# A hybrid decoder layer: the compression's position blocks become the stationary operand in fp32r halves, and the first norm sums by transposes

## The chip, the cores and the metric

The kernel runs on one core of one Trainium2 chip. The metric is the device time of one execution in microseconds (us); three runs of the kernel before gave 677.79, 677.90 and 678.41 us, so the median is 677.9. Engines are named as in the profile: PE (TensorE matmuls), PEld (TensorE weight loads), DVE (VectorE), ACT (ScalarE), POOL (GpSimd) and SP (SyncE, which only issues transfers here).

## What is computed

One decoder layer on a residual stream of 512 tokens and 1024 features in fp32. The first RMS norm feeds one large projection; its parts go to a pooling mixer, to a sparse attention with three key/value branches (compressed, selected, window) and to two merge gates; then come the output projection, a second norm and a gated MLP with a three-tap convolution. The change touches two places of it.

The norm:

```python
y = xf * lax.rsqrt(jnp.mean(xf * xf, axis=-1, keepdims=True) + RMS_EPS)
```

The compression, once for the keys and once for the values. A block is 32 consecutive tokens, a new block starts every 16, so there are 31 blocks of each of 2 groups:

```python
blk = kv[:, idx] + pe[None, None, :, None, :]
hid = jax.nn.silu(jnp.einsum('bnlgd,ldh->bngh', blk, w1))
return jnp.einsum('bngh,hd->bngd', hid, w2)
```

The sum over 32 positions of 64 features is a contraction over 2048 numbers; the kernel stores two positions on top of each other in the 128 partitions, which leaves 16 steps of 128 (position pairs). `w1` has 128 columns per step.

## The kernel before

**Precision.** Nearly all matmuls run on fp32r operands. A tensor is split by `split` into a rounded high half (an ACT copy to fp32r) and the rest (a DVE subtraction), and a product is three matmuls: high by high, high by low, low by high. A few small products stay plain fp32; the profile shows each of them as two MATMUL rows. Every MATMUL has a weight load (PEld) of its own.

**Stages.** The program begins with eight steps of the query/key projection (`round_a`), with the first norm's column sums made in between (`norm_rstd`, called at step 6 of 8). Then follow two streams that share all engines. The main stream "m" transposes queries and keys, computes the two compressions, the compressed attention and eight heads of attention. The filler stream "f" computes 22 feature tiles (`feature`: eight steps of three matmuls with 512 columns, "mm<-xh,whi", "mm<-xl,whi" and "mm<-xh,wlo" in the rows): two of them (`kv_in`) are the inputs of the compressions, the others feed the pooling mixer and the gates. After both streams come the output products and the MLP.

**Order.** All calls are recorded by `Plan` first. Each instruction gets a price (`Plan.price`, for a matmul its moving columns over 2250, at least 0.109 us), and a list scheduler searches for an order of the five engines in which PE, which takes its two streams each in their program order, has little to wait for. The order that it found is then emitted, and each engine runs it as it stands. A changed call can therefore move instructions that have nothing to do with it. Every instruction has line 434 in the profile (the line that emits), so the rows are told apart by tile names.

**First norm.** `square_x` adds the squares of the eight feature tiles into `acc` (128 features by 512 tokens). `norm_rstd` multiplies each 128-token slice of `acc` (stationary) by one column of ones, four plain fp32 matmuls with one moving column, and DVE turns the sums into `rstd` in 12 tiny steps.

**Compression.** `kv_in(i)` multiplies the feature tile by the broadcast norm into `kc` and adds the position table `pe` twice, once for the first half of a block's positions and once for the second: two tiles `kcb`, whose last axis is the position pair. Then, for 16 position pairs, a 128x128 piece of `w1` is stationary and the 62 block columns move, all plain fp32, into 62 columns of one bank. Tanh on ACT and one DVE step make `hid`, and a small matmul by `w2` follows (`compress_out`, "tr<-pr,hid").

## Time and profile before

| | |
|---|---|
| median of the three runs | 677.9 us |
| profiled execution | 678.3 us, of which its span 676.5 us |
| granted TensorE clock | 0.999 |
| PE / PEld busy in the span | 670.7 us / 610.1 us |
| DVE / ACT / POOL busy | 559.5 us / 467.3 us / 111.9 us |
| MATMUL rows | 4366 |

The span is cut by the profiler from the first to the last instruction. The rows of PE overlap, because a matmul's end is modelled: a row of 0.39 us may stand only 0.23 us after the one before. What a matmul costs PE is read from the distance of starts, or from a count of rows in a stretch in which PE never pauses. The two compressions lie at 71.8 to 75.4 us and 78.2 to 82.0 us, the first norm's sums at 30.7 to 31.5 us, and the two streams run until about 272 us.

### The profile page before, as it was taken

What the parts mean: (1) busy time and instruction counts of PE and PEld (TensorE: products, weight loads), DVE (VectorE), ACT (ScalarE), POOL (GpSimd) and SP (SyncE); (2) the same over time, 40 slices, a digit from 0 to 9 for tenths busy, and PEclk for the clock granted to TensorE, in tenths of its full rate; (3) what the DMA queues carried; (4) which work ended last, traced back from release to release, by engine and by line L of the source; (5) the groups of instructions that cost most, each with busy time, mean ns of one, the idle gap of its engine ahead of it and who ended that gap; (6) DMA issues with size and microseconds to landing.
All of it is one profiled execution on the core that took longest, in us unless ns stands there. A gap on an engine that the chain in (4) does not pass through costs nothing.

```text
span 676.5 us, 12188 instructions
## 1 busy us (share of the span) xinstructions
PE 670.7 (99%) x4366; PEld 610.1 (90%) x4366; DVE 559.5 (83%) x1246; ACT 467.3 (69%) x877; POOL 111.9 (17%) x138
## 2 busy tenths in 40 slices
PE   9999999999999999999999999999999999999998
PEld 8898888888888888988899999999999999999997
DVE  6869778788878867788888898888888989989883
ACT  7576577777677765447787867667766877776651
POOL 0010111010110110001322312222222322321121
PEclk9999999999999999999999999999999999999999
DMA  8468646454565555847878859777877888785574
GB/s 307 146 156 265 172 109 187 96 140 117 139 165 125 143 153 174 303 148 214 235 150 180 194 130 231 176 179 165 200 168 167 173 217 183 165 181 158 145 183 110
DMA packets 51180, 117.47 MB, mean 174 GB/s; under 512 B 5808, under 2 KB 9264, under 8 KB 51120
## 3 DMA queue, kind: packets, MB, share of 16 engines
q1 hardware_dynamic: 32112, 76.44, 35.5%
q0 software_dynamic: 18864, 40.12, 32.8%
q8 instruction: 34, 0.56, 0.3%
q14 instruction: 26, 0.21, 0.1%
q10 hardware_dynamic: 144, 0.14, 0.1%
HBM read 70.28 MB, written 6.29 MB: 113 GB/s over the span
## 4 chain that ended last, share of the span: by engine, by line
PE 93%; DMA 4%; issue 2%; DVE 0%; POOL 0%; ACT 0%; POOLq 0%
PE mm L434 39%; PE tr L434 33%; PE sc L434 11%; PE av L434 11%; DMA sl<-r 2%; DMA r<-wup 1%; DMA sl<-wraw 1%; DVE ft L434 0%; POOL sl L434 0%; ACT whi L434 0%; DVE wraw L434 0%; DVE s L434 0%; DVE o L434 0%; POOLq L434 0%; POOL ones L434 0%
## 5 line engine op out<-in xcount | busy, mean ns | idle before, releaser
L434 ACT ACTIVATE whi<-wraw 128x1024 fp32r<-128x1024 f32 (+4 forms) x99 | 91.7, 929 | 35.8 <-PE sc L434 14.2
L434 DVE TENSOR_TENSOR wlo<-wraw,whi 128x1024 fp32r<-128x1024 f32 (+3 forms) x73 | 73.9, 1016 | 4.4 <-ACT whi L434 3.7
L434 PE MATMUL tr<-tl,sh 128*128 128x256 f32 x261 | 73.2, 280 | 0.0
L434 PE MATMUL tr<-th,sl 128*128 128x256 f32 x250 | 70.5, 282 | 1.2 <-DMA sl<-r 1.2
L434 PE MATMUL mm<-xh,whi 128*128 128x512 f32 x176 | 70.8, 402 | 0.0
L434 PE MATMUL tr<-th,sh 128*128 128x256 f32 x250 | 70.5, 282 | 0.0
L434 PE MATMUL mm<-xh,wlo 128*128 128x512 f32 x176 | 68.8, 391 | 0.0
L434 PE MATMUL mm<-xl,whi 128*128 128x512 f32 x176 | 68.6, 390 | 0.0
L434 POOL DMA_DIRECT2D sl<-r x46 | 39.7, 863 | 143.9 <-ACT sl L434 109.6
L434 POOL DMA_DIRECT2D wlo<-wraw x26 | 22.3, 859 | 230.7 <-ACT wlo L434 178.6
L434 PEld LDWEIGHTS tr<-tl,sh 128*128 128x128 f32 x261 | 49.2, 189 | 0.2
L434 PEld LDWEIGHTS tr<-th,sl 128*128 128x128 f32 x250 | 47.0, 188 | 1.4 <-DMA sl<-r 1.4
L434 PEld LDWEIGHTS tr<-th,sh 128*128 128x128 f32 x250 | 47.0, 188 | 0.7 <-ACT tr L434 0.2
L434 ACT ACTIVATE wlo<-wraw 128x1024 fp32r<-128x1024 f32 x26 | 27.6, 1060 | 21.2 <-PE mm L434 19.7
L434 POOL DMA_DIRECT2D sl<-wraw x30 | 25.9, 864 | 87.3 <-ACT sl L434 64.7
L434 PEld LDWEIGHTS mm<-xh,wlo 128*128 128x128 f32 x176 | 33.0, 188 | 7.3
L434 PEld LDWEIGHTS mm<-xl,whi 128*128 128x128 f32 x176 | 33.1, 188 | 6.1
L434 PEld LDWEIGHTS mm<-xh,whi 128*128 128x128 f32 x176 | 33.1, 188 | 6.0
L434 ACT ACTIVATE sh<-wraw 128x512 fp32r<-128x512 f32 x56 | 34.8, 621 | 4.3 <-DVE wraw L434 4.0
L434 ACT ACTIVATE pp<-pp,asm 128x256 f32<-128x256 f32 (+3 forms) x64 | 35.4, 557 | 3.0 <-DVE asm L434 2.7
L434 DVE SCALAR_TENSOR_TENSOR ft<-fg,pr,ft 128x511 f32<-128x511 f32 (+1 forms) x44 | 32.9, 747 | 3.1 <-ACT ft L434 2.7
L434 ACT ACTIVATE sl<-r 128x512 fp32r<-128x512 f32 x46 | 28.6, 622 | 5.1 <-DMA r<-wdz 2.6
(451 smaller groups left out, 2179.8 us busy)
## 6 DMA issues: line engine op xcount, KB each, us to landing
wlo<-wraw POOLq DMA_DIRECT2D x26, 512.0 KB, 4.6
wraw<-wup SPq DMA_DIRECT2D x23, 512.0 KB, 4.2
sl<-r POOLq DMA_DIRECT2D x46, 256.0 KB, 5.3
wraw<-wf SPq DMA_DIRECT2D x22, 512.0 KB, 3.6
r<-wup SPq DMA_DIRECT2D x42, 256.0 KB, 5.3
sl<-wraw POOLq DMA_DIRECT2D x30, 256.0 KB, 4.6
wraw<-wdn SPq DMA_DIRECT2D x16, 320.0 KB, 3.9
sl<-s POOLq DMA_DIRECT2D x17, 256.0 KB, 5.4
```

The source lines that it names most:

```text
L434: getattr(self.real[o.eng], method)(*a, **kw)
```

## The change

In the first norm each of the four slices of `acc` is transposed by the identity instead (128 columns), and DVE sums the four groups of 128 columns and then goes on as before. The second norm keeps the matmuls by ones.

In the compression the operands change places. `kc` plus the first half of the position table is laid out with the position pair first and the 64 (group, 16-token half block) columns last, and split into fp32r halves that stand side by side: a stationary of 64 high and 64 low columns for each of 8 position pairs. The weights are laid out on the host so that pair l and pair l+8 stand side by side: 256 moving columns, split on the chip into high (`w1h`) and low (`w1l`). A matmul with 256 columns therefore gives four results at once: high and low halves of the blocks, each by the first-half and the second-half weights. Two matmuls (high weights, low weights) for each of 8 pairs make 16. The 128x256 result is copied out (`ab`), its two halves are transposed back, high and low parts are added, and the two half-block sums are added with a shift of one block. As only the first half of the position table was added, the difference for the second half (`dpe`) times the weights is summed on DVE (`dsum`, 8 steps of 128 columns) and reduced over the partitions by one matmul with ones. The prices of the plan are as they were.

```diff
-    def norm_rstd(acc_tile, dst, pt):
-        with pl.unit():
-            for t in range(NT):
-                PE.matmul(pt[:, t:t + 1], acc_tile[:, t * P:(t + 1) * P], ones[:, 0:1], start=True, stop=True)
+        if turn:
+            with pl.unit():
+                for t in range(NT):
+                    PE.transpose(pt[:, t * P:(t + 1) * P], acc_tile[:, t * P:(t + 1) * P], ident)
+            DVE.tensor_reduce(v[:, 1], pt.rearrange("p (t n) -> p t n", t=NT), axis=AX, op=ALU.add)
+            DVE.tensor_scalar(v[:, 0], v[:, 1], 1.0 / D, EPS, op0=ALU.mult, op1=ALU.add)
...
+            b = page("kcb", (P, 8, 64))
+            with pl.behind(flipped[1]):
+                DVE.tensor_add(b, kc.rearrange("p g (n l) -> p l (g n)", l=8),
+                               pe[:, i, 0:8][:, :, None].to_broadcast([P, 8, 64]))
             for a in range(2):
-                b = page("kcb", (P, 2, 32, 8))
-                with pl.behind(flipped[1]):
-                    DVE.tensor_add(b.rearrange("p g n l -> p (g n) l"), kc.rearrange("p g (n l) -> p (g n) l", l=8),
-                                   pe[:, i, 8 * a:8 * a + 8][:, None, :].to_broadcast([P, 64, 8]))
-                KC[i, a] = b
+                KC[i, a] = page("kcs", (P, 4, 2, 64), F32R)
+                split(KC[i, a][:, :, 0], KC[i, a][:, :, 1], b[:, 4 * a:4 * a + 4])
...
         pt = bank("tr")
+        more = page("dsum")
+        dsum, dpe = more[:, 0:P], more[:, P:P + 8]
+        DVE.tensor_sub(dpe, pe[:, i, 8:16], pe[:, i, 0:8])
         for q in range(4):
-            with pl.unit():
-                for l in range(4 * q, 4 * q + 4):
-                    PE.matmul(pt[:, 0:62], w1t[l // 4][:, (l % 4) * P:(l % 4 + 1) * P],
-                              KC[i, l // 8][:, :, l // 8:l // 8 + NB, l % 8], start=(l == 0), stop=(l == 15))
-        ph = pt[:, 0:62].rearrange("p (g n) -> p g n", g=2)
+            hi, lo = page("w1h", dt=F32R), page("w1l", dt=F32R)
+            split(hi, lo, w1t[q])
+            for l in range(2 * q, 2 * q + 2):
+                c = slice((l % 2) * 256, (l % 2 + 1) * 256)
+                x = w1t[q][:, (l % 2) * 256 + P:(l % 2 + 1) * 256]
+                if l:
+                    DVE.scalar_tensor_tensor(dsum, x, dpe[:, l:l + 1], dsum, op0=ALU.mult, op1=ALU.add)
+                else:
+                    DVE.tensor_scalar_mul(dsum, x, dpe[:, l:l + 1])
+                w = KC[i, l // 4][:, l % 4].rearrange("p s n -> p (s n)")
+                with pl.unit():
+                    for m in (hi, lo):
+                        PE.matmul(pt[:, 0:256], w, m[:, c], start=(l == 0 and m is hi), stop=(l == 7 and m is lo))
+        ab = page("ab")[:, 0:256]
+        ACT.activation(ab, pt[:, 0:256], AF.Copy)
+        pt = bank("tr")
+        with pl.unit():
+            for a in range(2):
+                PE.transpose(pt[:, a * P:(a + 1) * P], ab[:, a * P:(a + 1) * P], ident)
+            PE.matmul(pt[:, 256:257], dsum, ones[:, 0:1], start=True, stop=True)
+        low = page("ab")
+        halves = pt[:, 0:256].rearrange("p (a s n) -> p a s n", a=2, s=2)
+        lows, sums2 = (low[:, o:o + P].rearrange("p (a n) -> p a n", a=2) for o in (0, P))
+        ACT.activation(lows, halves[:, :, 1], AF.Copy)
+        ACT.activation(low[:, 320:321], pt[:, 256:257], AF.Copy)
+        DVE.tensor_add(sums2, halves[:, :, 0], lows)
...
+        DVE.scalar_tensor_tensor(ph, a4, low[:, 320:321], b4, op0=ALU.add, op1=ALU.add)
...
-                norm_rstd(acc, rstd2, bank("sc", (P, 2, T))[:, 0])
+                norm_rstd(acc, rstd2, bank("sc", (P, 2, T))[:, 0], False)
...
+    A["w1"] = A["w1"].reshape(2, P, 2, 8, P).transpose(0, 1, 3, 2, 4).reshape(2, P, 16, P)
```

The order moves with it, in three places. On PE, at the end of the sixth step of `round_a`, the four sums by ones become four transposes ("cs" holds the identity) in the same place:

```order
 L434 MATMUL sc<-wlo,xh 128x256 x4
-L434 MATMUL mm<-ones,acc 128x1 x4
+L434 MATMUL mm<-cs,acc 128x128 x4
 L434 MATMUL tr<-whi,xh 128x512 x3
 L434 MATMUL av<-whi,xh 128x512
```

Nothing else of PE moved there. In the whole first part of PE's order, up to the last key transpose before the compressions, this is the only difference.

On DVE, where the compressions begin ("kc" is the scaled feature tile, "qt" and "kt" are halves of transposed queries and keys for the main stream), before:

```order
L434 TENSOR_TENSOR qt<-tr,qt 64x512 x2
L434 TENSOR_TENSOR kc<-mm,rb 64x256 x4
L434 TENSOR_TENSOR kcb<-kc,pr 128x512 x2
L434 TENSOR_TENSOR qt<-tr,qt 64x512 x2
L434 TENSOR_TENSOR kc<-mm,rb 64x256 x4
L434 TENSOR_TENSOR kcb<-kc,pr 128x512 x2
L434 SCALAR_TENSOR_TENSOR hid<-hth,tr 128x2x31
L434 TENSOR_TENSOR kt<-tr,kt 64x512 x2
```

and now:

```order
L434 TENSOR_TENSOR kc<-mm,rb 64x256 x4
L434 TENSOR_TENSOR kcb<-kc,pr 128x512
L434 TENSOR_TENSOR qt<-tr,qt 64x512 x2
L434 TENSOR_TENSOR w1l<-w_399,w1h 128x512
L434 TENSOR_TENSOR kcs<-kcb,kcs 128x4x64
L434 TENSOR_TENSOR w1l<-w_400,w1h 128x512
L434 TENSOR_TENSOR w1l<-w_401,w1h 128x512
L434 TENSOR_TENSOR kcs<-kcb,kcs 128x4x64
L434 TENSOR_TENSOR kc<-mm,rb 64x256 x4
L434 TENSOR_TENSOR w1l<-w_402,w1h 128x512
L434 TENSOR_TENSOR kcb<-kc,pr 128x512
L434 TENSOR_SCALAR dsum<-w_399,dsum 128x128
```

The first `kc` now stands two `qt` steps earlier in DVE's order, and from it to the second `hid` there are 65 DVE instructions, where there were 27.

On PE the first compression before stands in one piece:

```order
L434 MATMUL mm<-xh,wlo 128x512
L434 MATMUL tr<-kcb,w_397 128x62 x4
L434 MATMUL tr<-kcb,w_398 128x62 x4
L434 MATMUL tr<-kcb,w_399 128x62 x4
L434 MATMUL tr<-kcb,w_400 128x62 x4
L434 MATMUL mm<-xh,whi 128x512
```

Now it begins one filler step (three matmuls) later, and pauses after its first four matmuls for four filler steps:

```order
L434 MATMUL mm<-xh,wlo 128x512
L434 MATMUL tr<-w1h,kcs 128x256
L434 MATMUL tr<-w1l,kcs 128x256
L434 MATMUL tr<-w1h,kcs 128x256
L434 MATMUL tr<-w1l,kcs 128x256
L434 MATMUL mm<-xh,whi 128x512
```

After the other twelve come eleven filler steps, the transposes and the sum of `dsum`, the second compression's sixteen matmuls in one piece, six filler steps, its transposes and the small product by the first `hid`, seven filler steps, and the product by the second `hid`. Before, four filler steps stood between the two compressions and four between the two products by `hid`. From there on the filler stream is ahead of where it was; after the last head five filler steps are left instead of twelve. From the output products on, PE's order is the same.

More of the change, by code (lines that the diff above doesn't have):

```diff
@@ L598, in hybrid_layer, with norm_rstd @@
     rb = keep("rb", (P, T))
-    def norm_rstd(acc_tile, dst, pt):
-        with pl.unit():
-            for t in range(NT):
-                PE.matmul(pt[:, t:t + 1], acc_tile[:, t * P:(t + 1) * P], ones[:, 0:1], start=True, stop=True)
+    def norm_rstd(acc_tile, dst, pt, turn):
         v = page("nrv", (P, 2, NT))
-        DVE.tensor_scalar(v[:, 0], pt[:, 0:NT], 1.0 / D, EPS, op0=ALU.mult, op1=ALU.add)
+        if turn:
[6 more added lines that the diff above has]
+            with pl.unit():
+                for t in range(NT):
+                    PE.matmul(pt[:, t:t + 1], acc_tile[:, t * P:(t + 1) * P], ones[:, 0:1], start=True, stop=True)
+            DVE.tensor_scalar(v[:, 0], pt[:, 0:NT], 1.0 / D, EPS, op0=ALU.mult, op1=ALU.add)
         rsqrt(dst, v[:, 0], v[:, 1])
@@ L629, in hybrid_layer @@
                 square_x(j)
-            norm_rstd(acc, rstd, bank("mm"))
+            norm_rstd(acc, rstd, bank("mm"), True)
             DVE.tensor_scalar_mul(rhalf, rstd, 0.5)
@@ L900, in hybrid_layer @@
         pt = bank("tr")
+        more = page("dsum")
+        dsum, dpe = more[:, 0:P], more[:, P:P + 8]
+        DVE.tensor_sub(dpe, pe[:, i, 8:16], pe[:, i, 0:8])
         for q in range(4):
-            with pl.unit():
-                for l in range(4 * q, 4 * q + 4):
-                    PE.matmul(pt[:, 0:62], w1t[l // 4][:, (l % 4) * P:(l % 4 + 1) * P],
-                              KC[i, l // 8][:, :, l // 8:l // 8 + NB, l % 8], start=(l == 0), stop=(l == 15))
-        ph = pt[:, 0:62].rearrange("p (g n) -> p g n", g=2)
+            hi, lo = page("w1h", dt=F32R), page("w1l", dt=F32R)
[5 more added lines that the diff above has]
+                    DVE.scalar_tensor_tensor(dsum, x, dpe[:, l:l + 1], dsum, op0=ALU.mult, op1=ALU.add)
+                else:
+                    DVE.tensor_scalar_mul(dsum, x, dpe[:, l:l + 1])
[6 more added lines that the diff above has]
+        pt = bank("tr")
+        with pl.unit():
+            for a in range(2):
[7 more added lines that the diff above has]
+        DVE.tensor_add(sums2, halves[:, :, 0], lows)
+        ph = low[:, 256:318].rearrange("p (g n) -> p g n", g=2)
+        a4, b4 = (sums2[:, a].rearrange("p (g n) -> p g n", g=2)[:, :, a:a + NB] for a in range(2))
+        DVE.scalar_tensor_tensor(ph, a4, low[:, 320:321], b4, op0=ALU.add, op1=ALU.add)
         hid = keep("hid", (P, 2, 32), bufs=2)
```

## The prediction

> **What bounds the kernel now.** I read the page first, then PE's waits, then the stretches around the changed places.
>
> ```profile
> PE 670.7 (99%) x4366; PEld 610.1 (90%) x4366; DVE 559.5 (83%) x1246; ACT 467.3 (69%) x877; POOL 111.9 (17%) x138
> ...
> PE 93%; DMA 4%; issue 2%; DVE 0%; POOL 0%; ACT 0%; POOLq 0%
> ...
> PE tr L434 <- DMA sl<-r: 1.2, 1, 1.2
> PE mm L434 <- POOL ones L434: 1.0, 1, 1.0
> PE sc L434 <- DMA sl<-wraw: 0.2, 1, 0.2
> ```
>
> The last three rows are all that PE waited for: 2.4 us of 676.5. PE makes 93% of the chain that ended last. So the time is the sum of what PE issues, and an edit gains what it takes from PE, as long as DVE and ACT still feed PE. They are the second thing to look at, above all where the compressions stand. The next rows are stretches of time, each with its length and then the busy time of PE, PEld, DVE, ACT and POOL:
>
> ```profile
> 66.00:96.00 30.00, 30.00 (x174) 25.62 (x173) 21.64 (x63) 20.30 (x42) 4.41 (x6) 1.00 0.51 125
> 96.00:255.00 159.00, 159.00 (x850) 134.35 (x849) 128.75 (x398) 117.16 (x254) 15.37 (x18) 1.00 0.56 143
> 544.00:561.00 17.00, 17.00 (x126) 16.14 (x125) 15.95 (x29) 13.84 (x25) 4.51 (x6) 1.00 0.86 201
> 646.00:663.00 17.00, 17.00 (x146) 17.00 (x145) 13.82 (x28) 8.62 (x16) 5.18 (x6) 1.00 0.78 173
> ```
>
> Around the compressions DVE is free for 8.4 of 30 us and ACT for 9.7; during the heads DVE is at 81%. In the third row, in the MLP, DVE is at 94% and PE still does not pause.
>
> **What PE loses and gains.** First the old pieces and the rows that price the new ones (PE in order of time: start, length, count):
>
> ```profile
> 30.69 0.95 PE L434 MATMUL mm<-ones,acc 128*128 128x1 f32 x8
> 31.50 0.94 PE L434 MATMUL tr<-whi,xh 128*128 128x512 f32 x3
> ...
> 32.98 0.86 PE L434 MATMUL tr<-whi,xl 128*128 128x512 f32 x3
> ...
> 40.46 0.29 PE L434 MATMUL mm<-bh,xh 128*128 128x280 f32 x1
> ...
> 41.48 0.29 PE L434 MATMUL mm<-bh,xl 128*128 128x280 f32 x1
> ...
> 59.09 0.60 PE L434 MATMUL tr<-cs,kp 128*128 128x128 f32 x4
> 59.53 0.60 PE L434 MATMUL tr<-cs,qp 128*128 128x128 f32 x4
> 59.88 0.48 PE L434 MATMUL mm<-xh,whi 128*128 128x512 f32 x1
> 60.20 0.39 PE L434 MATMUL mm<-xl,whi 128*128 128x512 f32 x1
> 60.43 0.39 PE L434 MATMUL mm<-xh,wlo 128*128 128x512 f32 x1
> ...
> 71.82 3.81 PE L434 MATMUL tr<-kcb,w 128*128 128x62 f32 x32
> 75.39 0.48 PE L434 MATMUL mm<-xh,whi 128*128 128x512 f32 x1
> 75.71 0.39 PE L434 MATMUL mm<-xl,whi 128*128 128x512 f32 x1
> ...
> 85.17 0.33 PE L434 MATMUL tr<-pr,hid 128*64 128x64 f32 x2
> ```
>
> A normal 512-column matmul takes 0.23 us from start to start (60.20 to 60.43). The eight rows of the norm's sums take 31.50 - 30.69 = 0.81 us, plus 0.08 that the group behind them is longer (0.94 against 0.86): 0.89 us, 0.11 each. Eight transposes take 60.20 - 59.09 - 0.23 = 0.88 us, again 0.11 each. Four transposes for eight such rows save 4 x 0.11 = **0.45 us**.
>
> One compression takes 75.39 - 71.82 = 3.57 us and makes the matmul behind it 0.09 longer (0.32 to the next start instead of 0.23): 3.66 us for 32 rows, 0.11 each, though only 62 columns move. So one, 62 and 128 moving columns cost the same here. For 256 columns the row of 646 to 663 us gives 17.00 / 146 = 0.116 us; that stretch holds the last output products, nothing but 256-column matmuls. The new compression is 16 x 0.116 = 1.86 us, two transposes and the two rows of one plain fp32 matmul with one column, 4 x 0.11 = 0.44, and 0.09 behind them: 2.39 us. Two compressions save 2 x (3.66 - 2.39) = **2.54 us**. Together PE issues 28 matmul rows and 3.0 us less. The price of the 16 is bounded by 0.11 from below and, if the doubled stationary or the changing bank cost something, by 0.13 from above (the 280-column products: eight starts from 40.46 to 41.48): 3.1 to 2.5 us.
>
> [...]
>
> **What DVE and ACT gain, and whether it is covered.** Prices, in groups by tile (busy time, mean ns of one, idle time before):
>
> ```profile
> L434 DVE TENSOR_TENSOR qt<-tr,qt 64x512 fp32r<-64x512 f32 x8 | 5.5, 689 | 0.4 <-ACT qt L434 0.2
> L434 DVE TENSOR_TENSOR kc<-mm,rb 64x256 f32<-64x256 f32 x8 | 3.4, 422 | 0.1
> L434 DVE TENSOR_TENSOR kcb<-kc,pr 128x512 f32<-128x512 f32 x4 | 2.6, 687 | 0.1
> L434 DVE TENSOR_TENSOR kp<-kp,gkv 128x256 f32<-128x256 f32 x4 | 1.5, 420 | 0.0
> 34.65 1.14 DVE L434 SCALAR_TENSOR_TENSOR diag<-cs,rstd,diag 128x128 fp32r<-128x128 f32 x4
> 39.74 1.28 DVE L434 TENSOR_REDUCE small<-qp 128x8 f32<-128x512 f32 x2 [2.70 <-ACT qp L434]
> 68.29 1.73 DVE L434 TENSOR_TENSOR kc<-mm,rb 64x256 f32<-64x256 f32 x4
> 82.33 0.22 DVE L434 TENSOR_SCALAR kcx<-tr 64x64 f32<-64x64 f32 x1 [4.25 <-PE tr L434]
> 59.29 1.06 ACT L434 ACTIVATE wlo<-wraw 128x1024 fp32r<-128x1024 f32 x1 [3.40 <-PE mm L434]
> 64.07 1.20 ACT L434 ACTIVATE qt<-tr 64x512 fp32r<-64x512 f32 x2
> L434 ACT ACTIVATE pwh<-pw 128x512 fp32r<-128x512 f32 x1 | 0.6, 624 | 0.0
> L434 ACT ACTIVATE hth<-tr 128x62 f32<-128x62 f32 x2 | 0.4, 223 | 4.7 <-PE tr L434 4.7
> ```
>
> In the norm DVE gets a reduction of 128x512 (0.64 by the row of two) ahead of its small steps, and 16-column work of 0.4 us. The row at 39.74 shows what covers them: DVE sits idle for 2.70 us before that point, where it waits for the projection's end. Cost nothing; without that cover 1.0 us.
>
> Per compression DVE loses one `kcb` (0.69) and gets two `kcs` (0.42 each), four `w1l` (0.69), eight `dsum` (1.14 / 4 = 0.285), one 128-column sum and one 62-column step (0.29 and 0.21): +5.7 us. ACT gets four `w1h` (0.62), two `kcs` and one `ab` (0.42 each, between the 62- and the 512-wide row) and two small copies (0.3 and 0.2): +4.3 us. Two compressions bring 11.4 us to DVE and 8.5 us to ACT, against 8.4 and 9.7 us that are free between 66 and 96. It does not fit there, and the new order answers by putting filler steps of 0.68 us in front of the late work. Whether the places suffice follows from the order and these durations, place by place:
>
> *First matmuls.* DVE's first `kc` stood at 68.29; two `qt` less before it (1.38) and the norm (0.45) put it at 66.5. Then 1.73 (`kc`), 0.69 (`kcb`), 1.38 (two `qt`), 0.69 and 0.42 make 71.4. PE comes there at 71.82 + 0.68 - 0.45 = 72.05: 0.6 us to spare. On ACT the first `w1h` falls into the 3.40 us of idle time before 59.29, so it stands at its two `qt` at 63.6 instead of 64.07; these (1.2), three 1024-wide steps (1.06), three `w1h` and a `kcs` follow, and its part is there at 70.3.
>
> *Fourth group.* PE is there 0.47 + 2.73 (four filler steps) + 0.93 later, at 76.2; DVE has two `w1l`, a `kcs`, the second `kc` and the last `w1l` to do, 4.2 us, and is done at 75.6.
>
> *Sum of `dsum`, second matmuls.* Its last matmuls, eleven filler steps (7.5 us) and the two transposes bring PE to 84.4. DVE has eight `dsum`, seven 512-wide steps and a `kcs` to do, 7.5 us, and is there at 83.1; the second compression's last weights follow 1.8 us later, at 84.9, and PE wants them at 86.2.
>
> *Second `hid`.* Six filler steps, the transposes and seven more bring PE to 96.2. DVE has 5 us to do until the first `hid` (90, wanted at 91.3) and 4.3 us from there to the second: 94.3. Before, PE was at that product at 85.2: the main stream starts its heads 11 us later.
>
> So everything is in time, by 0.6 to 1.9 us, with DVE hardly pausing for 25 us and ACT little more. The chain for the second `hid` has its seven filler steps (4.8 us) for three ACT and three DVE steps of 0.2 to 0.3 us each. Behind each late instruction on PE stands the filler stream as well as the main one, since PE takes its order as it stands, so a late DVE step costs its full lateness once. The spare times come from sums of means; I take **0.5 us** as lost here, with 0 and 2.5 us as ends (2.5: each of the five products late by 0.5 us).
>
> One price has no row: the new `kcb` reads `kc` with a step of eight elements in its innermost axis. `kc` itself reads with a step of two elements at the full rate (422 ns for 256 against 420 of `kp`). I bound it by nothing and by a doubling, +0.69 us per compression, and take nothing, the nearest row; the upper end makes the first place late by 0.1 us and eats the same from the two that follow.
>
> Sum against the profiled execution: 678.3 - 3.0 + 0.5 = 675.8. The median of the three runs lies 0.4 below it, so **675.4 us**.
>
> **Rivals.**
> *The spare time is not there.* DVE and ACT run full from 66 to 96 us, the five products come late by 0.5 us each, and the strided reads may double (2 x 0.69, of which 1.0 shows). For it: the sums above leave 0.6 us at the tightest place, and they are sums of means. Against it: the MLP runs with DVE at 94% and PE pauses 1.4 us in all. PE then waits 2.5 to 3.5 us, and the gain is gone: 677.4 to 678.4, no change. [...]
>
> *DVE bounds the heads.* The heads begin 11 us later and must share the rest with 11.4 us more DVE work in all; after them only five filler steps are left instead of twelve, so they end 7 x 0.68 - 3.0 = 1.8 us later than before. Their stretch shrinks by 9 us of some 175, and DVE goes from 81% to 85%. This decides from about 95%, the highest share that a row shows without a pause. If in-order DVE could not follow, PE would wait for as much as the stretch shrank: 675.4 + 9 = 684, or 680 if half of it shows; slower. Against it stands the row of 544 to 561.
>
> *Nothing is lost.* The order's spare times hold and 0.11 is the price: 677.9 - 3.1 = 674.8, and with the waits of 0.2 us and a few short ones gone 674.3.
>
> *The 256-column matmuls do not run at 0.116* because the stationary is used twice and loaded twice. At 0.227, as for 512 columns, the compression is 4.2 us and the two lose 1.0 us, the norm still gains 0.45: with the waits 679. Nothing in the trace hints at it.
>
> **How the numbers follow.** A measurement of this kernel can tell 0.2% (1.36 us) from no change: faster means under 676.5. My forecast with its losses of 0 to 1.5 us has 0.62; nothing lost 0.15; the spare time not there 0.16; DVE bounding the heads 0.05; the slow 256-column matmuls 0.02. The first two and a little of the third are faster: 0.77. Most of the third is no change: 0.17. The last two are mostly slower: 0.06. The range runs from 674.3 (nothing lost) to 677.4 (well into the third case) and leaves out about 0.17.
>
> **What would show it.** 4338 MATMUL rows; four transposes in 0.44 us near 30.7; 16 rows of 256 columns in about 1.9 us per compression, in pieces; DVE and ACT with almost no idle time between 66 and 96; PE's waits under 4 us in all, new ones on DVE tiles `kcs`, `w1l`, `dsum` or `hid`; the second product by `hid` near 96 us; from the output products on, all starts earlier by what was gained. If a new wait of more than 1.5 us stands before one of these products, or if the heads show DVE waits on PE again and again, the first or second rival holds. `kcb` rows of about 0.69 or 1.2 us settle the strided read.

## The result, and the profile after

The changed kernel takes 673.76 us (673.24 to 674.29), the kernel before 677.91 us (677.42 to 678.41) in runs beside it: a ratio of 0.9941, with a 95% interval of 0.9929 to 0.9952. The gain is 4.15 us, where 2.5 had been forecast, and 673.76 lies 0.5 us below the predicted range. A later pair on another occasion gave 674.17 against 677.20, 0.9947 (0.9930 to 0.9964): these medians lie 3.03 us apart, and the interval of the ratio reaches from 2.4 to 4.7 us. The profiled execution of the changed kernel took 673.75 us, its span is 672.0.

The page of the changed kernel, its busy times and its chain of waits, and then all that PE waited for in it:

```profile
PE 666.9 (99%) x4338; PEld 606.4 (90%) x4338; DVE 570.1 (85%) x1279; ACT 475.1 (71%) x895; POOL 112.2 (17%) x138
...
PE 99%; DMA 1%; SPq 0%; ACT 0%; DVE 0%; issue 0%
```

```profile
PE mm L434 <- POOL ones L434: 1.0, 1, 1.0
PE sc L434 <- ACT whi L434: 0.6, 1, 0.6
```

There are 4338 rows, 28 fewer than before, and PE is busy 3.8 us less. The chain went from 93% PE and 4% DMA to 99% and 1%: before, it ran through the transfers that held up the MLP (`sl<-r` for 1.2 us, `sl<-wraw` for 0.2), and these are gone from the list. No wait for `kcs`, `w1l`, `dsum` or `hid` has come in their place.

The changed places, on PE in order of time (start, length, count):

```profile
30.86 0.60 PE L434 MATMUL mm<-cs,acc 128*128 128x128 f32 x4
31.22 0.95 PE L434 MATMUL tr<-whi,xh 128*128 128x512 f32 x3
...
72.22 0.28 PE L434 MATMUL tr<-w1h,kcs 128*128 128x256 f32 x1
...
72.57 0.28 PE L434 MATMUL tr<-w1l,kcs 128*128 128x256 f32 x1
72.69 0.40 PE L434 MATMUL mm<-xh,whi 128*128 128x512 f32 x1
...
84.38 0.38 PE L434 MATMUL tr<-cs,ab 128*128 128x128 f32 x2
84.60 0.28 PE L434 MATMUL tr<-ones,dsum 128*128 128x1 f32 x2
84.74 0.36 PE L434 MATMUL tr<-w1h,kcs 128*128 128x256 f32 x1
...
91.28 0.33 PE L434 MATMUL tr<-pr,hid 128*64 128x64 f32 x2
96.53 0.33 PE L434 MATMUL tr<-pr,hid 128*64 128x64 f32 x2
```

The norm's transposes take 31.22 - 30.86 = 0.36 us, and the group behind them is 0.09 longer than its like, as the sums by ones had it. Four 256-column rows take 72.69 - 72.22 = 0.47 us, 0.118 each. The two transposes and the pair of one-column rows take 84.74 - 84.38 = 0.36.

The other side, DVE in order of time, shows by how much each piece was ahead of PE:

```profile
70.82 0.42 DVE L434 TENSOR_TENSOR kcs<-kcb,kcs 128x256 fp32r<-128x256 f32 x1
...
74.56 0.69 DVE L434 TENSOR_TENSOR w1l<-w,w1h 128x512 fp32r<-128x512 f32 x1
...
83.02 0.74 DVE L434 SCALAR_TENSOR_TENSOR dsum<-w,dsum 128x128 f32<-128x128 f32 x2
...
90.67 0.22 DVE L434 SCALAR_TENSOR_TENSOR hid<-hth,ab 128x62 f32<-128x62 f32 x1
...
95.40 0.22 DVE L434 SCALAR_TENSOR_TENSOR hid<-hth,ab 128x62 f32<-128x62 f32 x1 [0.57 <-ACT hth L434]
```

The first `kcs` is done at 71.24 and PE comes at 72.22; the fourth `w1l` is done at 75.25 and its product starts at 76.39; `dsum` is done at 83.76 and its product starts at 84.60; the two `hid` are done at 90.89 and 95.62, and PE is there at 91.28 and 96.53. Everything is in time, by 0.4 to 1.1 us.

Now where the 4.5 us between the two spans lie. I cut both programs at the same instructions on PE and take the distances of starts (in us; the last stage ends with the start of the last matmul):

| stage, by what PE starts | before | after | difference |
|---|---|---|---|
| start to the first norm's sums | 30.69 | 30.86 | +0.17 |
| norm's sums to the first "mm<-bh,xh" | 9.77 | 9.31 | -0.46 |
| from there over the compressions to the second norm's sums | 300.68 | 298.19 | -2.49 |
| second norm's sums to the last matmul | 331.73 | 329.82 | -1.91 |

The first stage differs from execution to execution (29.9 to 31.2 us over all profiles whose start is the same). The next two are the forecast's terms: -0.45 and -2.54. The last was forecast as nothing: in it PE's order is the same row by row, and it lost 1.9 us. (Behind the last matmul the changed kernel takes 0.2 us more, which makes the 4.7 us of the table the 4.5 of the spans.) These are the rows that bound it, before and after:

```profile
341.14 0.95 PE L434 MATMUL sc<-ones,acc 128*128 128x1 f32 x8
...
382.22 0.39 PE L434 MATMUL tr<-th,sl 128*128 128x256 f32 x1 [1.22 <-DMA sl<-r]
...
672.87 0.28 PE L434 MATMUL mm<-yth,sl 128*128 128x256 f32 x1
```

```profile
338.36 0.95 PE L434 MATMUL sc<-ones,acc 128*128 128x1 f32 x8
...
668.18 0.28 PE L434 MATMUL mm<-yth,sl 128*128 128x256 f32 x1
```

So two questions were left for the runs: is the arithmetic of the first three stages right for its own reasons, and why do the MLP's pauses go, with no instruction of any engine moved there?

### The profile page after: what moved, and what is told of

The parts are those of the page before. It is cut to its first block, busy times and chain, and to the rows that moved or that the text cites. A ratio compares the mean times of both kernels' runs of the same rounds, so it can differ in the third digit from the quotient of the medians.

```text
span 672.0 us, 12162 instructions
## 1 busy us (share of the span) xinstructions
PE 666.9 (99%) x4338; PEld 606.4 (90%) x4338; DVE 570.1 (85%) x1279; ACT 475.1 (71%) x895; POOL 112.2 (17%) x138
## 4 chain that ended last, share of the span: by engine, by line
PE 99%; DMA 1%; SPq 0%; ACT 0%; DVE 0%; issue 0%
PE mm L434 40%; PE tr L434 35%; PE sc L434 12%; PE av L434 11%; DMA wraw<-wa 1%; SPq L434 0%; ACT whi L434 0%; DVE o L434 0%
## 5 line engine op out<-in xcount | busy, mean ns | idle before, releaser
L434 ACT ACTIVATE pp<-pp,asm 128x128 f32<-128x128 f32 (+3 forms) x64 | 35.4, 556 | 5.9 <-DVE asm L434 5.7
L434 ACT ACTIVATE sh<-r 128x512 fp32r<-128x512 f32 x50 | 31.0, 620 | 2.1 <-ACT sh L434 0.9
```

The source lines that it names most:

```text
L434: getattr(self.real[o.eng], method)(*a, **kw)
```

## The experiments

Each label's expectation was written before it ran. "Last stage" below is the stage from the second norm's sums to the last matmul, read from each kernel's profile.

**The halves apart, and the kernel before once more.** The first runs repeat the kernel before, take the norm's hunk of the diff alone, and the compression's hunk alone:

```diff
-            norm_rstd(acc, rstd, bank("mm"))
+            norm_rstd(acc, rstd, bank("mm"), True)
```

The line above is the call in the norm alone, against the kernel before; the one below is the call in the compression alone, against the changed kernel.

```diff
-            norm_rstd(acc, rstd, bank("mm"), True)
+            norm_rstd(acc, rstd, bank("mm"), False)
```

> The kernel before, unchanged, to see whether its two pauses of PE in the MLP (about 1.6 us at 380.9 to 382.2 and about 0.4 us at 477 in the first profile, both behind a transfer into a low half) come again. Theory A (the pauses belong to this program, since its buffers and its relative times set them): they stand at the same products again, 1 to 2 us in all, and the time is 677.9. Theory B (they are chance in how long a transfer takes): they stand elsewhere or not at all, and the profiled time varies by the same 1 to 2 us.

> Only the first norm by transposes; the compression as before. By the rows of PE: eight rows of 0.11 us become four, 0.45 us less until the end of the two streams. Theory A (MLP pauses follow from the program's times and buffers): anything between 676 and 678, and the profile says which pauses are left. Theory B (pauses are chance): 677.5, the same as before. Rival: the reduction of 128x512 on VectorE ahead of the norm's small steps shows on PE; then no gain until the broadcast of the norm near 40 us.

> Only the compression with blocks stationary; the first norm by ones as before. By the rows of PE 2.3 us less until the end of the two streams. If the rest of the gain (1.4 us between the medians, behind the streams) belongs to the new order of the streams, the time is 674.2; if it needs both parts or is chance, 675.6.

The kernel before against itself: 1.0002 (0.9992 to 1.0012). Its second profile has the pauses at the same two products, but with other lengths:

```profile
PE mm L434 <- POOL ones L434: 1.0, 1, 1.0
PE sc L434 <- DMA sl<-wraw: 0.5, 1, 0.5
PE tr L434 <- DMA sl<-r: 0.3, 1, 0.3
```

So they belong to the program, and their size is not fixed: 1.2 us at the first product in one execution, 0.3 in the next. The norm alone: 676.23 us, 0.9985 (0.9976 to 0.9995). The compression alone: 674.25 us, 0.9955 (0.9942 to 0.9969). The stage that begins with the first norm's sums takes 9.30 us with the norm alone and 9.78 with the compression alone, which takes 2.56 us from the stage that holds it (300.68 to 298.12). That is the forecast's arithmetic, each term in its place, to 0.02 us. Both kernels gain more in the whole than there, because their last stage is shorter as well: 330.36 and 330.20 us, against 331.73 and 331.21 in two profiles of the kernel before.

**The plan's price.** A plain fp32 matmul is two rows (8 for the four of the second norm's sums, 0.95 us) but is priced as one; the words of the change say that the prices stayed. The kernel before with the true price:

```diff
-            return max(n / 2250.0 + (0.005 if n < 300 else 0.0), 0.109), 0.17, 0
+            twice = 2 if method == "matmul" and a[1].dtype == F32 else 1
+            return twice * max(n / 2250.0 + (0.005 if n < 300 else 0.0), 0.109), 0.17, 0
```

> The kernel before, with one change: the plan prices a plain fp32 matmul at two passes (0.218 us at least, as its two rows take) instead of one. Same instructions, another order. If the gain beyond PE's rows came from a plan that fits the chip better, since the new compression has no badly priced matmuls, this is faster than before by up to 1.4 us: 676.5. If not, 677.9 within 0.5. If order alone moves the time by chance, it may also be slower by about 1.

It took 679.58 us, 1.0038 (1.0018 to 1.0059), slower; its runs spread from 677.45 to 684.92, and the profiled one, of 677.98, is among the fastest, so the profile does not show where the median's loss lies. Its last stage of 331.86 us has the pause for `sl<-r` (0.7 us) and one of 0.9 us that waits for DVE (`x`). That the old compression was priced at half its cost did not hide a gain in the order.

**Once more, padded, and short.** Then the changed kernel again, beside two kernels that separate "new order" from "less work on PE". The padded one is the changed kernel with each of the 32 new matmuls issued a second time, unpriced (the plan takes the added calls at no cost), so that no engine's order moves. The short one is the kernel before with every second of the 16 position pairs left out, priced as if they were there; its compressed branch sums half the positions only.

```diff
+                    pl.unpriced = True
+                    for m in (hi, lo):
+                        PE.matmul(pt[:, 256:512], w, m[:, c], start=False, stop=(l == 7 and m is lo), skip_group_check=True)
+                    pl.unpriced = False
```

```diff
-                for l in range(4 * q, 4 * q + 4):
+                for l in range(4 * q, 4 * q + 4, 2):
```

> The changed kernel again, on the same chip and beside the same runs of before as the next three. Theory B (the pauses of PE in the MLP are chance of one execution, and the PE rows of the change are the whole lasting gain): the ratio comes out nearer to 0.9956 (3.0 us) than to 0.9941, and the time from the second norm to the end is spread between 329.5 and 331.5 us from profile to profile. Theory A (the pauses belong to the program): again 4 us less than before, and again 329.8 us from the second norm on.

> The changed kernel with each of its 32 new 256-column matmuls issued twice, the second time into the unused half of the bank and without a price in the plan, so that the order of all engines stays as it is: PE gets 32 x 0.116 = 3.7 us more. If the gain behind the streams came from being earlier by 3 us, it goes: 678.6 and 331 us from the second norm on. If it belongs to the new order, or is chance: 673.8 + 3.7 = 677.5, with 329.8 us (order) or anything from 329.5 to 331.5 (chance) from the second norm on. The rows of the doubled matmuls also test the price of 0.116 us.

> The kernel before with every second position pair of the compressions left out (so the compressed branch is not the reference's) and the plan's prices made up, so that the order of all engines stays as before: 32 rows of 0.114 us, 3.65 us less on PE. If being earlier by 3 us removes the pauses of the MLP: 677.5 - 4.9 = 672.6, with 329.8 us from the second norm on. If the pauses belong to the old order: 677.5 - 3.65 = 673.9, with 331.2 to 331.7. If they are chance: 673.9 on the median, any of these in the profile.

The changed kernel repeats its gain (0.9947, above), with a last stage of 330.07 us; whether the gain is the whole 4.15 us or the 3.0 us of the rows, this pair does not tell. The short kernel takes 672.95 us, 0.9933 (0.9918 to 0.9948): 3.64 us of its gain lie where the 32 rows were (216.70 to 213.06 us up to the last attention product with the values), and its last stage is 330.18 us, with the old order on all engines. The padded kernel takes 678.35 us, 1.0013 (1.0002 to 1.0024): the 32 rows cost 222.85 - 219.01 = 3.84 us, 0.120 each, and its last stage is 331.27 us, with the new order. PE's waits of the padded kernel:

```profile
PE mm L434 <- POOL ones L434: 1.0, 1, 1.0
PE tr L434 <- DMA sl<-r: 0.9, 1, 0.9
PE sc L434 <- DMA sl<-wraw: 0.4, 1, 0.4
```

These are the two pauses of the kernel before, in the new order; the short kernel, in the old order, has neither. So by these two profiles the pauses do not hang on the order, nor on what the compression does. They went with PE being some 3 us earlier, or with it having some 30 rows fewer.

**How much spare time there is.** The changed kernel with two more DVE steps (0.69 us each) on each `kcb`, unpriced. PE's order is unchanged; ACT takes one `ab` ahead of a `kcs`:

```diff
+            pl.unpriced = True
+            for _ in range(2):
+                DVE.tensor_tensor(b, b, b, op=ALU.max)
+            pl.unpriced = False
```

> The changed kernel with two more VectorE steps of 128x512 on each of the two kcb tiles (0.69 us each, a maximum of the tile with itself), unpriced, so that PE's order stays. It measures the spare time of the compression's chain. By the profile of the changed kernel the places have 1.0, 1.1, 0.8, 1.0, 0.4 and 1.0 us to spare, and VectorE idles 0.7 us once between them: 1.4 us more before the first and 2.8 before the last should show 0.4 us on PE at the first matmuls and 1 to 1.5 us in all: 675.3. If the filler stream or other waits hide it: 673.8. If VectorE bounds the heads, the whole 2.8 us or more: 676.6.

It took 675.06 us, 0.9957 of the kernel before (0.9938 to 0.9977), 0.9 us more than the changed kernel in the same runs. Of 2.77 us that were added, PE lost 220.69 - 219.01 = 1.68, with two waits that the changed kernel doesn't have:

```profile
PE tr L434 <- DVE dsum L434: 0.4, 1, 0.4
PE tr L434 <- DVE kcs L434: 0.4, 1, 0.4
```

By the distances of starts the products stand 0.6 us (first `kcs`), 0.7 us (first `dsum`) and 0.4 us (second `dsum`) later than in the changed kernel; the list counts only the time in which PE is idle. So 1.1 us were covered, about 0.5 per compression, and the rest of the lateness showed. The last stage was 329.59 us.

**Later, with as few rows.** With four such steps instead of two everything behind the compressions comes later than in the kernel before, with the changed kernel's 4338 rows. Its counterpart is the kernel before, earlier, with its 4366 rows: 28 of the correction products (high by low, low by high) of the two compressed features on half their columns, so half the tokens of these two features go without that correction.

```diff
-            for _ in range(2):
+            for _ in range(4):
```

```diff
-                PE.matmul(pt, wh[:, c], xl[k], start=False, stop=False)
-                PE.matmul(pt, wl[:, c], xh[k], start=False, stop=(k == nk - 1))
+                PE.matmul(pt[:, h:], wh[:, c], xl[k][:, h:], start=False, stop=False, skip_group_check=True)
+                PE.matmul(pt[:, h:], wl[:, c], xh[k][:, h:], start=False, stop=(k == nk - 1), skip_group_check=True)
```

> The changed kernel with four added VectorE steps of 128x512 (they take each block's maximum with itself; 0.69 us each in the run with two) on each of the two kcb, outside the plan's prices: TensorE's order and its 4338 rows are the changed kernel's, and the results too, but everything behind the compressions comes later by the added steps less the spare time: between 1.68+1.38=3.1 us (if only the second block counts) and 1.68+2.77=4.4 us, so that the second norm's sums lie at 341.5 to 342.8, where the kernel before had them at 341.1. Theory A, the pauses of the multilayer perceptron go with when its transfers fall in time: they come back, the stage behind the second norm's sums takes 331.2 to 331.8 us instead of 329.8, and the time is 678.1 to 679.6. Theory B, the pauses go with TensorE's number of instructions ahead of them (28 more in the kernel before, so that its code is fetched at other places): they stay away, the stage takes 329.6 to 330.1 and the time is 676.8 to 678.1.

> The kernel before with 28 of the correction products of the two compressed features on 256 of their 512 columns, priced as before, so that the order on every engine and TensorE's 4366 rows are those of the kernel before; left out is the correction of half the tokens of those two features. 28 rows fall from 0.227 to 0.118 us: TensorE is 3.05 us earlier at the compressions, as in the changed kernel. Theory A (when the transfers fall in time): the pauses go, the stage behind the second norm's sums falls from 331.2 to 331.9 to 329.8 to 330.4, the time is 677.2-3.05-1.3=672.9, with 672.4 to 673.4. Theory B (TensorE's number of instructions): the pauses stay, the stage takes 331.2 to 331.9 and the time is 677.2-3.05=674.2.

The delayed kernel took 679.66 us, 1.0032 (1.0020 to 1.0045). It is later by more than expected: its second norm's sums start at 344.34, 6.0 us behind the changed kernel's. The steps alone don't do that: of the 5.5 us that were added, 4.2 show at the two products that wait for `kcs` and `dsum`, 2.1 each by the distances of starts. Another 1.5 us come right behind the second of them, where the granted clock is 0.50 from 89.8 to 93.2 us and the 256-column rows stand 0.21 us apart instead of 0.12. All five runs have a mean clock of 0.997, where the changed kernel's have 0.999 or 1.000; why the clock fell there is not shown. But its last stage is 330.17 us and its waits hold no transfer:

```profile
PE tr L434 <- DVE dsum L434: 1.9, 1, 1.9
PE tr L434 <- DVE kcs L434: 1.8, 1, 1.8
PE mm L434 <- POOL ones L434: 1.0, 1, 1.0
PE sc L434 <- ACT whi L434: 1.0, 1, 1.0
```

Being 3.2 us later than the kernel before did not bring the pauses back. That overshoots the place that was aimed at, but the other kernels speak against theory A as well: the sums start at 340.01 us in the kernel with two steps, which has no pause, and at 339.94 us with the norm alone, which has one. The narrow kernel took 676.47 us, 0.9995 (0.9984 to 1.0005), and does not tell much by its earliness, because only 0.9 of the 3.05 us arrived: PE waited 1.1 us for `qp` and others took the rest. Its last stage is 331.51 us, as in the kernel before; where 1.22 us were lost at `tr<-th,sl` it lost nothing, but 0.9 us at the product that waits for `sl<-wraw`, where the kernel before had lost 0.2.

**Both norms by transposes.** The version that might have beaten both kernels:

```diff
-                norm_rstd(acc, rstd2, bank("sc", (P, 2, T))[:, 0], False)
+                norm_rstd(acc, rstd2, bank("sc", (P, 2, T))[:, 0], True)
```

> The changed kernel with the second norm's sums by transposes too. Its eight 1-column rows of 0.89 us give way to rows of 0.44 us, as at the first norm (9.77 to 9.30 us): 0.45 us less of TensorE, 673.9-0.45=673.5. The VectorE reduction that takes their place (0.68 us at the first norm) delays the scale of the MLP's gates, which TensorE reaches about 6 us later behind other products, so it is hidden. The rival: the plan puts VectorE's steps in another order from some 40 us ahead of the norm to the end, and the pauses of the MLP, which move with when its transfers fall, come back in part: 674.0 to 675.5.

It took 679.89 us, 1.0041 (1.0027 to 1.0055). One more DVE step ahead of the gates made the plan put DVE's work in another order from 277 us to the end, and PE's waits are new ones. The profile is of the slowest of its six runs, 684.65 us:

```profile
PE tr L434 <- ACT u L434: 5.0, 4, 3.2
PE av L434 <- DMA sl<-r: 2.1, 1, 2.1
```

What the transposes may gain, this version lost many times over; that the reordering did it is argued from these waits, as no run has the one without the other.

**The slow read.** The changed kernel with `kc` written position by position, so that `kcb` reads it in one run:

```diff
-                    DVE.tensor_mul(kc[q * 64:(q + 1) * 64, g], pt[g * 64:(g + 1) * 64, q::2],
-                                   rb[g * 64:(g + 1) * 64, q::2])
+                    DVE.tensor_mul(kc[q * 64:(q + 1) * 64, :, g * 32:(g + 1) * 32].rearrange("p l n -> p n l"),
+                                   pt[g * 64:(g + 1) * 64, q::2].rearrange("p (n l) -> p n l", l=8),
+                                   rb[g * 64:(g + 1) * 64, q::2].rearrange("p (n l) -> p n l", l=8))
```

> The changed kernel with kc written position by position, so that kcb reads it contiguously; TensorE's order is unchanged. If the step of 32 bytes in kcb's read is what took its 1.16 us, kcb falls to 0.69 us, and the strided write of kc stays near its 0.42 us or rises above it. The time stays within 0.2% of the changed kernel's (672.6 to 675.2) if the spare time covered the slow read; if it cost time, up to 0.9 us is won: 673.0.

The two views by tile, first of the changed kernel and then of this one (durations min/median/max, first and last start):

```profile
L434 DVE TENSOR_TENSOR kc<-mm,rb x8: 409/422/428, 65.8 to 74.1; 64x256 f32<-64x256 f32 x8
L434 DVE TENSOR_TENSOR kcb<-kc,pr x2: 1132/1155/1178, 67.6 to 75.2; 128x512 f32<-128x512 f32 x2
```

```profile
L434 DVE TENSOR_TENSOR kc<-mm,rb x8: 621/630/642, 66.1 to 75.5; 64x256 f32<-64x256 f32 x8
L434 DVE TENSOR_TENSOR kcb<-kc,pr x2: 683/688/693, 68.7 to 76.8; 128x512 f32<-128x512 f32 x2
```

The read is what cost `kcb` 1.16 us; without its step of 32 bytes it takes 0.69. But now `kc` writes with a step of 256 bytes and takes 0.63 instead of 0.42, and per compression DVE spends 4 x 0.63 + 0.69 = 3.21 us instead of 4 x 0.42 + 1.16 = 2.84. The time is 674.50 us, 0.9963 (0.9949 to 0.9977), which can't be told from the changed kernel's.

**Where the instruction packets fall.** What was left was the number of PE's rows. The profile's list of DMA queues has one for instructions; here of the kernel before (packets, MB, share):

```profile
q8 instruction: 34, 0.56, 0.3%
```

That is 16.5 KB a packet, one for each 128 of the 4366 rows (4366 / 34); with 100 more rows, in a run below, there are 35. No view names the engine that they are for. I read them as PE's, as they keep step with its rows: in the kernel before and the changed one 96 to 156 rows stand between two packets, but 24 to 77 of DVE's instructions. In the changed kernel, with 28 rows fewer ahead, they fall further on in the same work: the first three behind the second norm's sums stand 61, 214 and 320 rows behind them, where they stood at 30, 150 and 306. In the kernel before, one stands between 361 and 362 us; the list of queues for that microsecond alone:

```profile
q8 instruction: 1, 0.02, 6.0%
```

And what SP does there in the kernel before, and at the same place of the work in the changed one (start, length, count):

```profile
361.84 2.03 SPq L434 DMA_DIRECT2D r<-wup  x2
```

```profile
357.88 0.90 SPq L434 DMA_DIRECT2D r<-wup  x2
```

The issue of these two transfers takes 1.1 us longer in the kernel before, and the chain from the second (`r`, then `sl<-r` at 373.74, then the product at 382.22) is the one that ends in the pause. To move the packets without a change of any work, rows of warm-up (ones on ones, as the program begins anyway) were added at the start, unpriced, with n = 50 or 64 plain fp32 matmuls (100 or 128 rows) on the kernel before and n = 14 (28 rows) on the changed kernel:

```diff
+    pl.unpriced = True
+    for i in range(n):
+        PE.matmul(pt[:, 0:P], ones, ones, start=(i == 0), stop=(i == n - 1))
+    pl.unpriced = False
```

> The kernel before with 100 more rows of warm-up (50 plain fp32 products of ones on ones, unpriced) at its start, so that every later instruction of TensorE stands 100 rows further on; the order is that of before on all engines. The profile counts packets of instructions on a DMA queue of their own, and on TensorE's side one comes every 128 rows: 306 rows behind the second norm's sums in the kernel before, 320 in the changed one, which differ by 28 rows; 28 fewer and 100 more are the same place in a period of 128. Theory B (the pauses go with where TensorE's instruction packets fall): the stage behind the second norm's sums falls from the 331.2 to 331.9 us of the kernels with 4366 and 4370 rows to the 329.6 to 330.4 of those with 4334 to 4342, though everything comes 11 to 22 us later by the time of the rows. Theory C (the pauses go with the old instruction count or with chance, not with that place): it stays at 331.2 to 331.9. The whole time is that of before plus 11 to 22 us, less what the start had to wait for anyway.

> The changed kernel with 28 more rows of warm-up at its start: its later instructions stand where those of the kernel before stand, in a stream of 4366 rows. Theory B: the pauses come back, the stage behind the second norm's sums rises from 329.8 to 331.2 to 331.9 us. Theory C and the run with VectorE's added steps (later by 5.8 us, no pauses): it stays at 329.6 to 330.4. The whole time is the changed kernel's plus 3.1 to 6.2 us for the rows, and 1.3 to 1.7 us more by theory B.

> The kernel before with 128 more rows of warm-up, a whole period of the instruction packets, as a control to the run with 100: 28 rows apart from it, and with packets that fall as in the kernel before. Theory B: the pauses stay, 331.2 to 331.9 us behind the second norm's sums. If this stage falls to 329.6 to 330.4 here as well, what took the pauses away with 100 rows was not the packets' place.

With 100 rows the kernel before took 686.54 us: 10.09 us more at the start and 329.48 us in the last stage. All that PE waited for:

```profile
PE mm L434 <- POOL ones L434: 1.0, 1, 1.0
```

With 128 rows it took 690.76 us: 13.55 us more at the start and 330.65 us in the last stage, with pauses of 0.3 and 0.2 us at the old products. And the changed kernel with 28 rows took 677.17 us, 1.0001 of the kernel before (0.9991 to 1.0011): 2.18 us more at the start and 332.42 us in the last stage, with these waits:

```profile
PE sc L434 <- DVE x L434: 1.1, 1, 1.1
PE mm L434 <- POOL ones L434: 1.0, 1, 1.0
PE tr L434 <- DMA sl<-r: 0.3, 1, 0.3
PE tr L434 <- ACT tr L434: 0.2, 1, 0.2
```

The wait for `sl<-r` is an old one; the longest, for DVE's `x`, is not a transfer and stands at a product at which the kernel before did not wait.

All the profiles but that of the twofold norm, whose order differs, by the place of the first packet behind the second norm's sums. The last column is what PE lost at the two old products together (`tr<-th,sl` and `sc<-yth,sl`), by the distance of their starts from the matmuls ahead of them, less 0.12 us each:

| first packet, rows behind the sums | kernels | last stage, us | mean | lost at the two products, us |
|---|---|---|---|---|
| 29 to 34 | before 331.73 and 331.21; new price 331.86; padded 331.27; narrow 331.51; norm alone 330.36; changed + 28 rows 332.42; before + 128 rows 330.65 | 330.36 to 332.42 | 331.38 | 0.7 to 1.8 |
| 48 to 80 | changed 329.82 and 330.07; compression alone 330.20; short 330.18; slack 329.59; delayed 330.17; contiguous read 330.86; before + 100 rows 329.48 | 329.48 to 330.86 | 330.05 | 0.0 to 0.2 |

By the length of the last stage the two groups differ by 1.3 us and touch (330.36 and 330.65 against 330.86), because other waits come and go in it; so a single length does not tell them apart, and the 128-row control fell 0.55 us short of what was expected of it. By what was lost at the two old products they don't touch, and the three runs with added rows all fall as theory B says: 0.0 us with 100 rows, 0.8 with 128, and 0.7 in the changed kernel with 28.

Whole runs give less than the profiles. From each kernel's gain in the medians, against the kernel before beside it, take what its first stages up to the second norm's sums gained (for the changed kernel 4.15 - 0.46 - 2.49 = 1.2 us; with added rows the longer start counts as a loss of these stages). What is left is 1.2 and 0.1 us for the two measurements of the changed kernel, 0.4 for the compression alone, 0.6 short, 0.8 slack, 0.4 delayed, 0.0 contiguous read and 0.7 with 100 rows: 0.5 on average. In the other group it is 0.6 with the norm alone, -0.3 padded, -0.2 narrow, -0.1 with 128 rows and -0.8 for the changed kernel with 28 rows: -0.2 on average, and -2.2 under the new price. Few of these figures are clear of noise by themselves (the intervals of the ratios are 0.7 us and more to each side, and the start stage, which stands in those with added rows by one profile each, varies by 1.3 us). Together they have the sign of theory B, with about 0.7 us where 1.3 to 1.7 were expected.

## Why the prediction was wrong

*PE bounds the kernel; the time is the sum of what it issues.* Right for the stages that hold the change: each gave what its rows promised.

*The norm, -0.45 us.* Right: -0.46 in the changed kernel, -0.47 with the norm alone.

*The compressions, -2.54 us, with 0.116 us for a 256-column row.* Right: 0.118 and 0.120 us were measured, and 2.49 us were gained in the stage, 2.56 with the compression alone. One-, 62- and 128-column rows cost the same 0.11 us here, each with a weight load of its own (the page counts 4366 of both before and 4338 after).

*The loss of 0.5 us to late DVE and ACT work.* Wrong as a term: at most 0.05 us were lost. The place-by-place sums gave PE to some tenths (72.22 for 72.05 at the first products, 96.53 for 96.2 at the second `hid`) and DVE less well (first `kcs` 71.24 for 71.4, `dsum` 83.76 for 83.1, second `hid` 95.62 for 94.3): `kcb` took 1.16 us and a `dsum` step in a row 0.385, where 0.69 and 0.285 had been priced. (The doubling of 0.69, by which the strided read had been bounded, no run shows: `kcb` took 0.47 us more.) So each place had spare time, but 0.4 to 1.1 us of it where 0.6 to 1.9 had been promised. The sums left a spare time at every place, and I still took half a microsecond off, without a place for it. The run with two added steps shows that some 0.5 us per compression was in fact left.

*"From the output products on, all starts earlier by what was gained."* This is the step that failed. Behind it stood that the MLP's pauses, 1.2 and 0.2 us by the list of PE's waits, stay what they are. In the profiles the last stage fell by 1.9 us, against the second profile of the kernel before by 1.4. In the medians of this result it is 1.2 us, and without it the time would have been 677.91 - 2.95 = 674.96, inside the range; in the later pair (3.03 us) it is 0.1, so how much of it lasts is open. The rival "Nothing is lost" came nearest: it let the waits of 0.2 us go and ended at 674.3, but kept the one of 1.2.

The sum again with what was measured: 678.3 - 0.46 - 2.49 - 1.91 + 0.17 = 673.6, where the profiled execution took 673.75.

*Why the pauses went.* Not by the new order, which has them when it is padded; and not because all starts earlier, as far as the delayed kernel and the starts of 339.94 and 340.01 us show. They follow the place of PE's instruction packets: in the profiles 28 rows more brought them to the changed kernel, 100 took them from the kernel before, 128 did not. A packet has 16.5 KB, and there is one for 128 rows on average, each a matmul and its weight load. What goes with its place here is 0.7 to 1.8 us at two products in single profiles, and about 0.7 us of 675 by whole runs. How a packet delays a transfer is not shown. The late second issue on SP is there in the kernel before, in the padded one, under the new price and with 128 rows (1.0 to 2.8 us between the two issues), and in none of the eight profiles of the other group at this place (0.5 us each). But four profiles with packets in the old place have pauses and no late issue (the kernel before again, the narrow one, the norm alone and the changed one with 28 rows), so it is at most one of the ways. What the runs show is that rows which do no work, far ahead of the pauses, go with their coming and going, one profile for each; that it is the packets themselves that hold up a transfer is argued from their period and that one place, and stays open.

The other rivals fell: DVE did not become the bound of the heads (no wait for it there), the 256-column rows ran at 0.118 us, and the spare time held.

## What to carry to other kernels

When one engine makes the whole chain, count its rows, price them by stretches in which it does not pause, and work out spare times place by place: a loss needs a place. Leave them a margin, as they came out up to 1 us shorter here than summed. Short waits for transfers in the profile of the kernel before are not a constant of the program; a kernel whose instruction count ahead of them changes may lose or gain a microsecond of them (here the same two products lost 0.0 to 0.2 us in one group of profiles and 0.7 to 1.8 in the other), so they belong into the range, on both sides. A gain of that kind should not be credited to the edit: work-free rows at the start can tell the two apart. And a stage that differs in one profile of each kernel (1.9 us here) should be held against the medians of whole runs (1.2 and 0.1 us) before it is explained.

## What was not expected of the hardware

A DVE read of fp32 numbers 32 bytes apart took 1.16 us for 128x512 where a run of neighbours took 0.69, and a write 256 bytes apart 0.63 us for 64x256 where 0.42 was the price of neighbours. The read is at 1.7 times the time of neighbours, the write at 1.5; why is not shown.

Scalar-tensor-tensor steps of 128x128 in a row stood further apart where each reads what the one ahead of it wrote. A single row is 0.35 us long in both cases, but four independent ones (`diag`) start 0.26 us apart, which gave the 0.285 of the prediction (1.14 / 4), and five chained ones (`dsum`) 0.385 us. No run separates the chain from the other operands.

```profile
86.25 1.90 DVE L434 SCALAR_TENSOR_TENSOR dsum<-w,dsum 128x128 f32<-128x128 f32 x5
```

PE's instruction packets, one every 128 rows on average, go with 0.7 to 1.8 us lost at two products that wait for transfers, by where they fall; with the packets elsewhere these products lose at most 0.2 us.

In the delayed kernel PE waited about 2 us ahead of 74.4 us and again ahead of 88.9 us, and from 89.8 to 93.2 us the granted clock was 0.50.
